# Two-layer hybrid mixer on one core: two-stream h slots, a new tile order in the first layer, earlier conversion of y

## The chip, the cores and the metric

The kernel runs on one core of a Trainium2 chip. The metric is the device time of one execution in microseconds (us). The profile is one execution taken apart by the hardware profiler: when each engine worked (TensorE = PE, VectorE = DVE, ScalarE = ACT, GpSimd = POOL, SyncE = SP) and which semaphore ended each wait.

## The reference

Two layers over two token streams of 256 tokens each, a context stream (s = 0) and a latent stream (s = 1), with model width 2048. Only the latent stream of the second layer is an output, so there the context needs keys and values alone.

```python
for l in range(DEPTH):                       # DEPTH = 2
    h  = layernorm(x)  * (1 + scale)   + shift        # latent, 256 x 2048
    hx = layernorm(ctx)* (1 + scale_x) + shift_x      # context
    qa, ka, va, za, qb, kb, vb, zb, qkv_c, zc, ab = split(h @ w_in)   # and the same of hx
    ya = attention(rope(rms(qa)), rope(rms(ka)), va; context keys first) * silu(za)   # 8 heads, 2 kv heads
    yb = neighbourhood_attention(qb, kb, vb, rpb) * silu(zb)                          # 4 heads
    yc = rms(bidirectional_gated_deltanet(conv(qkv_c), ab)) * silu(zc)                # 4 heads
    x  = layernorm(alpha * x + gate * (concat(ya, yb, yc) @ w_out))
    # context alike, but not in the last layer
```

## The kernel before

**Tiles.** `w_in` is cut in tiles of 128 columns, named by group and head: `("ck", 0)`, `("za", 3)`. A layer has 52 of them. The activations lie transposed, 16 pieces (`kt`) of 128 features by 512 tokens, context in columns 0 to 255 and latent in 256 to 511. To keep fp32 accuracy, each operand is two parts: a rounded high part and the rest. ACT (or DVE, by `high`) casts the high part, and DVE subtracts to get the low one (`wHL<-raw,wHL` in the rows). Each product is three matmuls: high by high, high by low, low by high. So a tile over both streams is 16 x 3 = 48 matmuls of 512 columns (`acc<-hH,wHL` and `acc<-hL,wHL`).

**Layers.** In the first layer (l = 0) all 52 tiles are of 512 columns. In the second, 32 tiles serve the latent stream alone (`LAT_ONLY`; 48 matmuls of 256 columns each) and 20 "shared" tiles (ck, cv, ka, va, kb, vb) serve both; there the two streams' h lie in different buffers of the ring `hp`, so `run_w` issues 96 matmuls of 256 columns for a shared tile. The tiles run in the order of `ORDER[l]`; behind each, a task (`evac`) takes it out of PSUM, and further tasks work on it: `attend` (scores, softmax, product with v, product with the gate's silu in `y`), and `delta` (the DeltaNet head: its triangular inverse in 31 dependent steps, a scan, the norm, and the product with silu(zc)).

**Output.** `convert` makes the high and low part (`yHL`) of each of the 16 finished heads y in the order `K_ORDER[l]`; 0 to 7 are A heads, 8 to 11 B, 12 to 15 the DeltaNet heads. `run_wo` then multiplies them with `w_out` in column blocks nb of 512: the `o<-wHL,yHL` matmuls, three for each head, block of 128 tokens and nb. The normalised result is h of the next layer.

**Order of work.** A program at build time, class `Order`, steps all tasks by a model of each engine's time and so writes out one fixed order of instructions for each engine. Each engine then works strictly in its order. `mod_dve` is filler on DVE: 512 products (`gvj<-gvl,xsb,modT` and `gvl<-…`) for the second layer's modulation, issued where the model finds DVE free. Weights come on the SP queue as `raw`; the bias tables `tbm` and the gate rows `gscr<-mrow` go through POOL's queue, `tbm` behind `gscr<-mrow`.

The end of the last weight tile in the main loop, before the change:

```python
if it[2] == ORDER[l][-1]:
    for k in range(4):
        hp.put(2)
    if it[3][1] == KT:
        if l == 0:
            layer_params(1)
        od.spawn(convert(l))
```

A tile runs as four groups of four kt (`it[3]` is the range of kt, `KT` is 16), so `convert` starts behind the last group. `md<-gvr,xs` is a modulation product that stands between the last tile and the first output matmul in both layers.

Of the kernel before, what the change touches and what calls it, by code (L numbers as in the profile page):

```python
# [7 lines left out]
F32 = mybir.dt.float32  # L8
# [8 lines left out]
KT = 16  # L17
# [47 lines left out]
def _b(*hs):  # L65
# [9 lines left out]
    [("ck", 0), ("cv", 0), ("cq", 0), ("ka", 0), ("ka", 1), ("zc", 0), ("va", 0), ("va", 1)] + _REST,  # L75
# [5 lines left out]
    [12, 0, 1, 2, 13, 3, 4, 5, 6, 14, 7, 8, 9, 15, 10, 11],  # L81
# [179 lines left out]

class Eng:
# [60 lines left out]
def hybrid_grid_flow(  # L323
# [15 lines left out]
    hp = Ring(od, big, "h", 32)  # L339
    yq = Ring(od, big, "yq", 18)  # L340
# [145 lines left out]
    def split_ahead(force=None):  # L486

        low_parts(force)
        while pos["split"] < len(queue):
            it = queue[pos["split"]]  # L490
            if it[0] in ("w", "wo"):
# [5 lines left out]
                if it[0] == "wo" and it[1] == DEPTH - 1 and it[3] == 3:  # L497
                    rings += [P_r, hp]
# [211 lines left out]
    for l in range(DEPTH):  # L710
        L[l] = dict(hs={}, xn={}, ln_ok=[Flag() for _ in range(4)], gates=Flag(), h_lat=Flag(), y={}, yp={}, yh={}, y_ok={})
# [12 lines left out]
    def h_run(l, streams, xn, ab_ps, wab):  # L724

        hs, mt = L[l]["hs"], modT[l]
# [7 lines left out]
        def turn():  # L734
# [11 lines left out]
            a = yield from hp.get("hH", dt=F32R)  # L746
            b = yield from hp.get("hL", dt=F32R)
            high(a, hf)
            V.tensor_tensor(b, hf, a.bitcast(F32), op=ALU.subtract)
            for i, kt in enumerate(kts):  # L750
                if both:
                    hs[kt] = [(slice(0, 512), a, b)]
                    hfs[kt] = hf
                else:
                    s, c = streams[0], slice(i * 256, i * 256 + 256)
                    hs.setdefault(kt, []).append((slice(s * 256, s * 256 + 256), a[:, c], b[:, c]))
                    hfs[kt] = hf[:, c]
# [313 lines left out]
    def attend(l, kind, h, q, rs, tbm=None):  # L1071
# [3 lines left out]
        while not (kk in P and vk in P and yk in P["y"]):  # L1075
            yield 1.0
        k, v, yt = P[kk], P[vk], P["y"][yk]
# [5 lines left out]
        left = [len(units)]  # L1083
        qs, ks, vs = (q, k, v) if two else ((q,), (k,), (v,))
        pairs = ((0, 0), (1, 0), (0, 1))[:3 if two else 1]

        def soft(tts, out):
# [6 lines left out]
            for i, t in enumerate(tts):  # L1094
                for n, (a, b) in enumerate(pairs):
                    T.matmul(sc[:, i * nk:(i + 1) * nk], qs[a][:, t * 128 - q0:t * 128 - q0 + 128], ks[b][:, 0:nk],
                             start=(n == 0), stop=(n == len(pairs) - 1))
            yield
# [27 lines left out]
        def one(tts):  # L1126
# [50 lines left out]
            yield  # L1177
            c = slice(tts[0] * 128 - y0, tts[0] * 128 - y0 + w)
# [3 lines left out]
            if not left[0]:  # L1182
                yq.put(2 if two and not l else 1)
                P["y_ok"][yk] = 1
# [36 lines left out]
    def delta(l, h):  # L1221
# [146 lines left out]
        for i in range(31):  # L1368
# [6 lines left out]
            yield 0  # L1375
            V.tensor_tensor(R[:, i + 1:32, 0:c_], R[:, i + 1:32, 0:c_], t, op=ALU.add)
            yield 0
# [158 lines left out]
        yield  # L1536
        pt = yield from tr.get("otr")
# [3 lines left out]
        while 12 + h not in P["y"]:  # L1541
            yield 1.0
        yt = P["y"][12 + h]
# [27 lines left out]
    def run_w(it):  # L1571
# [3 lines left out]
        if k0 == 0:  # L1575
# [7 lines left out]
            {c[0].start // 256 for c in P["hs"].get(k, ())} >= (set(streams) if l else {0})  # L1583
# [32 lines left out]
    def convert(l):  # L1616
        P = L[l]
        for n, k in enumerate(K_ORDER[l]):
# [38 lines left out]
    def run_wo(it):  # L1657
# [25 lines left out]
        def mults(s, i, yt, wh, wl, first, last_):  # L1683
            c = slice(i * 128, i * 128 + 128)
            ps = op["ps", nb, s][i]
            T.matmul(ps, yt[:, 0, c], wh, start=first, stop=False)
            T.matmul(ps, yt[:, 1, c], wh, start=False, stop=False)
            T.matmul(ps, yt[:, 0, c], wl, start=False, stop=last_)
# [14 lines left out]
        else:  # L1703
            w_free(it)
            if nb == 3:
                hp.put()
# [324 lines left out]
```

## Time and profile before

| | |
|---|---|
| time before, 3 runs | 1749.89, 1753.56 and 1754.09 us, median 1753.56 us |
| profiled execution: its own time | 1746.19 us |
| its span (first to last instruction) | 1744.4 us |
| mean granted TensorE clock | 0.99 of full |
| PE busy | 1664.7 us (95%) |
| DVE busy | 1307.4 us (75%) |
| ACT busy | 856.0 us (49%) |
| DMA | 296.43 MB, mean 170 GB/s |

The first layer's tiles run to about 846 us, its output matmuls to about 1053 us, the second layer's tiles to 1630 us, and its output matmuls to the end. "Busy" of matmuls is modelled and overlaps from one matmul to the next, so the price of one matmul is better read from the distance between starts in an unbroken run.

### The profile page before, as it was taken

To read this page: it belongs to the slowest core of one execution; us is meant where nothing else is said; L and a number is where in the kernel's file an instruction comes from. 1 tells how busy PE (TensorE), PEld (TensorE's weight loads), DVE (VectorE), ACT (ScalarE), POOL (GpSimd) and SP (SyncE) were. 2 spreads that over 40 slices of the span, in tenths; PEclk is the share of its full clock that TensorE was granted. 3 is DMA by queue.
4 is the path that set the end of the run, shared out by engine and by line. 5 is a ranking of instruction groups with operands and counts; after the bars stand their busy time and mean duration, and the time that the engine had idled before them with its cause. 6 is when DMAs were issued, how large, how long until landed. Compare 5 with 4: busy or idle time off the path is not lost. (4 is left out here: it accounts for less than half of the span.)

```text
span 1744.4 us, 32868 instructions
## 1 busy us (share of the span) xinstructions
PE 1664.7 (95%) x11487; PEld 1390.7 (80%) x11487; DVE 1307.4 (75%) x3948; ACT 856.0 (49%) x1932; POOL 42.7 (2%) x112
## 2 busy tenths in 40 slices
PE   4999999999999999999899898999999999999896
PEld 1667778787787878877688677898999899999785
DVE  5346787988798987868886788658788777685667
ACT  2225455364555443534444465545675655545443
POOL 0000100000000000000000000000000000000000
PEclk9999999999999999999999999999999999999998
DMA  9993544554455555454557767345454534353475
GB/s 322 347 348 100 158 144 120 164 166 146 125 157 161 162 153 171 135 178 127 165 182 231 254 222 217 98 128 146 130 163 139 149 98 141 114 159 119 145 233 182
DMA packets 213493, 296.43 MB, mean 170 GB/s; under 512 B 38384, under 2 KB 104656, under 8 KB 213328
## 3 DMA queue, kind: packets, MB, share of 16 engines
q1 hardware_dynamic: 211632, 291.07, 54.8%
q0 software_dynamic: 1696, 3.27, 0.6%
q8 instruction: 90, 1.47, 0.3%
q14 instruction: 75, 0.61, 0.1%
HBM read 287.88 MB, written 6.37 MB: 169 GB/s over the span
## 5 line engine op out<-in xcount | busy, mean ns | idle before, releaser
L307 PE MATMUL acc<-hH,wHL 128*128 128x256 f32 (+1 forms) x3968 | 1026.4, 338 | 8.8 <-DVE wHL L288 5.7
L307 PEld LDWEIGHTS acc<-hH,wHL 128*128 128x128 f32 x3968 | 683.1, 190 | 108.9 <-issue 26.4
L307 PE MATMUL acc<-hL,wHL 128*128 128x256 f32 (+1 forms) x1984 | 651.2, 328 | 0.2 <-DVE hL L288 0.2
L288 DVE TENSOR_TENSOR wHL<-raw,wHL 128x512 fp32r<-128x512 f32 (+1 forms) x610 | 403.0, 672 | 86.4 <-ACT wHL L288 71.9
L288 ACT ACTIVATE wHL<-raw 128x512 fp32r<-128x512 f32 (+1 forms) x524 | 311.1, 611 | 209.4 <-PE o L307 59.0
L307 PEld LDWEIGHTS acc<-hL,wHL 128*128 128x128 f32 x1984 | 378.3, 191 | 31.3 <-issue 3.4
L307 PE MATMUL o<-wHL,yHL 128*128 128x512 f32 x1152 | 275.1, 397 | 11.4 <-DVE yHL L288 4.8
L307 PEld LDWEIGHTS o<-wHL,yHL 128*128 128x128 f32 x1152 | 217.6, 191 | 62.9 <-DVE wHL L288 6.9
L288 DVE CUSTOM_DVE_ANT_0 gvl<-gvl,xsb,modT 128x256 f32<-128x256 f32 x224 | 109.5, 489 | 11.9 <-DMA xsb<-xsd 6.9
L288 DVE CUSTOM_DVE_ANT_0 gvj<-gvl,xsb,modT 128x256 f32<-128x256 f32 x224 | 107.3, 479 | 7.1 <-DMA xsb<-xsd 5.4
L307 PE MATMUL md<-gvr,xs 128*32 128x128 f32 (+1 forms) x1408 | 88.7, 350 | 24.7 <-DMA gvr<-in_w_mod_dram 24.0
L288 ACT ACTIVATE P<-P,zz 128x512 f32<-128x512 f32 (+1 forms) x61 | 39.4, 658 | 98.4 <-DVE zz L288 98.4
L307 PEld LDWEIGHTS md<-gvr,xs 128*32 128x32 f32 x1408 | 33.0, 113 | 64.5 <-DMA gvr<-in_w_mod_dram 27.8
L288 DVE TENSOR_TENSOR Xt<-X,R 128x60 f32<-128x60 f32 (+24 forms) x248 | 52.3, 211 | 9.4 <-ACT X L288 3.9
L288 DVE TENSOR_TENSOR R<-R,Xt 128x60 f32<-128x60 f32 (+24 forms) x248 | 52.8, 213 | 5.8
L307 PE MATMUL pv<-PT,v 128*128 128x128 f32 (+1 forms) x288 | 52.0, 296 | 0.0
L288 DVE SCALAR_TENSOR_TENSOR cv<-acc,cw,cv 128x510 f32<-128x510 f32 (+1 forms) x48 | 33.7, 703 | 22.3 <-ACT cv L288 21.3
L288 DVE TENSOR_REDUCE mx<-sc 128x1 f32<-128x512 f32 (+1 forms) x60 | 41.2, 687 | 6.3 <-PE sc L307 5.5
L307 PEld LDWEIGHTS pv<-PT,v 128*128 128x128 f32 x288 | 42.3, 191 | 3.5 <-ACT P L288 0.4
L288 DVE DVE_READ_ACCUMULATOR2_ANT modT<- 128x1 f32 x512 | 43.5, 85 | 0.0
L288 ACT ACTIVATE PT<-ptr 128x512 f32<-128x512 f32 (+1 forms) x54 | 32.1, 594 | 22.9 <-PE ptr L317 22.5
L288 ACT ACTIVATE P<-sc,nb,rqs 128x512 f32<-128x512 f32 (+1 forms) x48 | 33.6, 703 | 15.7 <-DVE nb L288 15.3
(294 smaller groups left out, 1783.6 us busy)
## 6 DMA issues: line engine op xcount, KB each, us to landing
raw<-in_w_in_dram SPq DMA_DIRECT2D x398, 256.0 KB
gvr<-in_w_mod_dram SPq DMA_DIRECT2D x256, 256.0 KB
raw<-in_w_out_dram SPq DMA_DIRECT2D x176, 256.0 KB
gvl<-in_w_modt_dram SPq DMA_DIRECT2D x256, 128.0 KB
raw<-in_w_in_dram SPq DMA_DIRECT2D x36, 128.0 KB
xp<-in_xin_dram SPq DMA_DIRECT2D x16, 256.0 KB
E<-growd SPq DMA_DIRECT2D x16, 256.0 KB
xres<-in_xin_dram SPq DMA_DIRECT2D x16, 256.0 KB
```

What stands on the lines that cost most here:

```text
L288: r = fn(*a, **k)
L307: r = self.real.matmul(out, lhsT, rhs, **k)
```

## The change

It does these things:

1. `ORDER[0]` is rewritten: B heads stand among the first layer's middle tiles, A heads 4 to 6 behind them, and the last tiles are qa7, za7, zc3, so two gates are last. `K_ORDER[0]` follows.
2. In layer 1 the h of both streams lies in one set of 32 slots `hv` (class `Slots`, each half of a slot booked by itself), context in columns 0 to 255 and latent in 256 to 511; a shared tile is then 48 matmuls of 512 columns. `convert` writes the parts of y into freed slots of the same set. A ring `Spare` over slots 16 to 31 takes the place of `hp` for the last output weights.
3. `h_run` writes high and low parts kt by kt: in layer 1 two pieces of 256 columns in place of one of 512.
4. `attend` no longer waits for its gate's y before the scores, only before the last product, and frees y's ring entry once the scores are issued.
5. In the inverse of `delta`, the product and the addition of a step are issued as a pair.
6. `delta` waits for its gate before it takes the PSUM tile of the transposes `otr`, and no longer behind them.
7. `convert` starts behind the first of the last tile's four groups.

```diff
 ORDER = (
-    [("ck", 0), ("cv", 0), ("cq", 0), ("ka", 0), ("ka", 1), ("zc", 0), ("va", 0), ("va", 1)] + _REST,
+    [("ck", 0), ("cv", 0), ("cq", 0), ("ka", 0), ("ka", 1), ("zc", 0), ("va", 0)]
+    + _a(0, 1, 2) + _c(1) + _a(3) + [("zc", 1)] + _b(0) + _c(2) + _b(1) + [("zc", 2)] + _b(2) + _c(3) + _b(3) + [("va", 1)] + _a(4, 5, 6)+ [("qa", 7), ("za", 7), ("zc", 3)],
     [("cq", 0), ("zc", 0), ("za", 0), ("zc", 1), ("za", 1), ("za", 2), ("ck", 0), ("cv", 0), ("ka", 0), ("va", 0)]
     + [("ka", 1), ("va", 1)]
     + [k for k in _REST if k not in [("zc", 1), ("za", 0), ("za", 1), ("za", 2)] + _KV1],
 )
 K_ORDER = (
-    [12, 0, 1, 2, 13, 3, 4, 5, 6, 14, 7, 8, 9, 15, 10, 11],
+    [12, 0, 1, 2, 13, 3, 8, 9, 14, 10, 11, 4, 5, 6, 15, 7],
     [12, 0, 1, 2, 13, 3, 4, 5, 6, 14, 7, 8, 9, 10, 11, 15],
...
+class Slots:
+
+
+    def __init__(self, order, n):
+        self.order, self.t = order, [None] * n
+        self.busy, self.times = set(), {}
+
+    def take(self, keys):
+        self.busy.update(keys)
+
+    def get(self, keys):
+        while True:
+            t = max(self.times.get(k, 0.0) for k in keys)
+            if any(k in self.busy for k in keys):
+                yield Want(self, keys)
+            elif t > self.order.t["PE"]:
+                yield ("at", t)
+            else:
+                return self.take(keys)
...
-            a = yield from hp.get("hH", dt=F32R)
-            b = yield from hp.get("hL", dt=F32R)
-            high(a, hf)
-            V.tensor_tensor(b, hf, a.bitcast(F32), op=ALU.subtract)
+            if both:
+                h2 = []
+                for nm in ("hH", "hL"):
+                    h2.append((yield from hp.get(nm, dt=F32R)))
+            else:
+                yield from hv.get([(2 * kt + j, streams[0]) for kt in kts for j in range(2)])
+            cols = slice(streams[0] * 256, streams[-1] * 256 + 256)
+            w = cols.stop - cols.start
             for i, kt in enumerate(kts):
-                if both:
-                    hs[kt] = [(slice(0, 512), a, b)]
-                    hfs[kt] = hf
-                else:
-                    s, c = streams[0], slice(i * 256, i * 256 + 256)
-                    hs.setdefault(kt, []).append((slice(s * 256, s * 256 + 256), a[:, c], b[:, c]))
-                    hfs[kt] = hf[:, c]
+                hfs[kt] = hf[:, i * w:i * w + w]
+                P["ht"][kt] = h2 if both else hv.t[2 * kt:2 * kt + 2]
+                high(P["ht"][kt][0][:, cols], hfs[kt])
+            for kt in kts:
+                a, b = P["ht"][kt]
+                V.tensor_tensor(b[:, cols], hfs[kt], a[:, cols].bitcast(F32), op=ALU.subtract)
+                hs[kt] = hs.get(kt, set()) | set(streams)
...
-        while not (kk in P and vk in P and yk in P["y"]):
+        while not (kk in P and vk in P):
             yield 1.0
-        k, v, yt = P[kk], P[vk], P["y"][yk]
+        k, v = P[kk], P[vk]
...
+            scored[0] -= len(tts)
+            if not scored[0]:
+                yq.put(2 if two and not l else 1)
...
+            while yk not in P["y"]:
+                yield 0.3
+            yt = P["y"][yk]
...
                 op=ALU.mult,
             )
-            yield 0
             V.tensor_tensor(R[:, i + 1:32, 0:c_], R[:, i + 1:32, 0:c_], t, op=ALU.add)
-            yield 0
+            if i % 1 == 0:
+                yield 0
...
+        while 12 + h not in P["y"]:
+            yield 0.5
+        yt = P["y"][12 + h]
         pt = yield from tr.get("otr")
         for n in range(n0, 4):
             T.transpose(pt[:, blk[n]], o2[:, blk[n]], ident)
         tmp.put()
-        while 12 + h not in P["y"]:
-            yield 1.0
-        yt = P["y"][12 + h]
...
-            parts = [c for c in P["hs"][kt] if l == 0 or c[0].start // 256 in streams]
-            for i, (c, a, b) in enumerate(parts):
-                T.matmul(ps[:, c], wh[:, w], a, start=(kt == 0 and i == 0), stop=False)
-                T.matmul(ps[:, c], wh[:, w], b, start=False, stop=False)
-                T.matmul(ps[:, c], wl[:, w], a, start=False,
-                         stop=(kt == KT - 1 and i == len(parts) - 1))
+            a, b = (t[:, lo:512] for t in P["ht"][kt])
+            T.matmul(ps[:, lo:512], wh[:, w], a, start=(kt == 0), stop=False)
+            T.matmul(ps[:, lo:512], wh[:, w], b, start=False, stop=False)
+            T.matmul(ps[:, lo:512], wl[:, w], a, start=False, stop=(kt == KT - 1))
...
-                t = yield from hp.get("yHL", dt=F32R, shape=[128, 2, 256])
                 c = slice(s * 256, s * 256 + 256) if l == 0 else slice(0, 256)
-                high(t[:, 0], y[:, c])
-                V.tensor_tensor(t[:, 1], y[:, c], t[:, 0].bitcast(F32), op=ALU.subtract)
+                if l == 0:
+                    if s:
+                        for j in range(2):
+                            hv.t[2 * n + j] = yield from hp.get("hv", dt=F32R)
+                    yield from hv.get([(2 * n + j, s) for j in range(2)])
+                    t = [hv.t[2 * n + j][:, c] for j in range(2)]
+                else:
+                    yield from hv.get(hv.whole(n))
+                    t = [hv.t[n][:, 0:256], hv.t[n][:, 256:512]]
+                high(t[0], y[:, c])
+                V.tensor_tensor(t[1], y[:, c], t[0].bitcast(F32), op=ALU.subtract)
...
-                for k in range(4):
-                    hp.put(2)
-                if it[3][1] == KT:
-                    if l == 0:
-                        layer_params(1)
+                if l == 0:
+                    hp.put(8)
+                else:
+                    hv.put([k for i in range(2 * it[3][0], 2 * it[3][1]) for k in hv.whole(i)])
+                    if it[3][1] == KT:
+                        spare.open(od.t["PE"])
+                if it[3][0] == 0:
                     od.spawn(convert(l))
+                if it[3][1] == KT and l == 0:
+                    layer_params(1)
```

**PE, a shared tile of the second layer.** `abtok` and `ab` are small products of the gates; `acc` is the tile. Before:

```order
L307 MATMUL acc<-hH,wHL 128x256 x2
L307 MATMUL acc<-hL,wHL 128x256
L307 MATMUL acc<-hH,wHL 128x256
L307 MATMUL abtok<-cst,abpart 128x16 x4
L307 MATMUL acc<-hH,wHL 128x256
L307 MATMUL acc<-hL,wHL 128x256
L307 MATMUL acc<-hH,wHL 128x256 x2
```

Now:

```order
L367 MATMUL acc<-hv,wHL 128x512 x18
L367 MATMUL ab<-hf,wab 32x256 x4
L367 MATMUL acc<-hv,wHL 128x512 x6
L367 MATMUL abtok<-cst,abpart 128x16 x4
L367 MATMUL acc<-hv,wHL 128x512 x24
```

In place of 96 matmuls of 256 columns a shared tile has 48 of 512; over the 20 shared tiles that is 1920 before and 960 now.

**PE, the end of the first layer's tiles.** `otr` are the transposes of the last DeltaNet head's output `o`, `ptr` and `pv` the transposes of an attention head's probabilities and their product with v, `sc` scores. Before:

```order
L307 MATMUL md<-gvr,xs 32x256 x4
L307 MATMUL sc<-kb,qb 128x512
L317 MATMUL otr<-cst,o_9450 128x128 x4
L307 MATMUL o<-wHL,yHL 128x512 x12
L307 MATMUL sc<-kb,qb 128x512
L307 MATMUL sc<-kb,qb 128x256 x2
L307 MATMUL o<-wHL,yHL 128x512 x9
L317 MATMUL ptr<-cst,P 128x128 x4
```

Now:

```order
L367 MATMUL md<-gvr,xs 32x256 x4
L377 MATMUL ptr<-cst,P 128x128 x4
L367 MATMUL pv<-PT,v 128x256 x2
L377 MATMUL otr<-cst,o_9458 128x128 x4
L367 MATMUL o<-wHL,hv 128x512 x645
L377 MATMUL htr<-cst,res 128x128 x8
```

The scores of the last B head are gone from here; the last piece of a head's attention (`ptr`, `pv`) stands between `md` and `otr`, and behind `otr` come output matmuls alone.

**ACT at the same place, now.** `se` are the three steps of the last gate's silu, `PT` the copy of `ptr` that `pv` reads, `o_9458` the operand of `otr`:

```order
L348 ACTIVATE hv<-y 128x256 x4
L348 ACTIVATE wHL<-raw 128x512
L348 ACTIVATE ory<-orv 128x4
L348 ACTIVATE ory<-ory 128x4
L348 ACTIVATE se<-acc 128x512
L348 ACTIVATE se<-se,cst 128x512
L348 ACTIVATE se<-se 128x512
L348 ACTIVATE PT<-ptr 128x512
L348 ACTIVATE o_9458<-O,c_osc 128x128 x4
```

The conversions `hv<-y` now come ahead of the last gate's silu, and the PT copy and the operand of `otr` behind it.

**PE, the end of the second layer's tiles.** `sc` are the last B head's scores. Before:

```order
L307 MATMUL md<-gvr,xs 32x256 x4
L307 MATMUL o<-wHL,yHL 128x512 x3
L307 MATMUL sc<-H,qb 128x512 x2
L307 MATMUL sc<-L,qb 128x512
L307 MATMUL sc<-H,qb 128x512 x2
L307 MATMUL sc<-L,qb 128x512
L307 MATMUL o<-wHL,yHL 128x512 x42
```

Now:

```order
L367 MATMUL md<-gvr,xs 32x256 x4
L367 MATMUL o<-wHL,hv 128x512 x21
L367 MATMUL sc<-H,qb 128x512 x2
L367 MATMUL sc<-L,qb 128x512
L367 MATMUL sc<-H,qb 128x512 x2
L367 MATMUL sc<-L,qb 128x512
L367 MATMUL scan<-vw,E 128x128 x2
L367 MATMUL o<-wHL,hv 128x512 x36
L377 MATMUL ptr<-cst,P 128x128 x4
```

Twenty-one output matmuls now stand ahead of the scores, where three stood.

**DVE at the same place, now.** `mrow` goes to POOL's queue, `tbm` comes from it; `wHL` rows are low parts of weights:

```order
L348 TENSOR_TENSOR hv<-y,hv 128x256 x3
L348 TENSOR_TENSOR wHL<-raw,wHL 128x512
L348 SCALAR_TENSOR_TENSOR rr<-scan,g_neg_eg_12468,vn 128x128 x2
L348 TENSOR_TENSOR wHL<-raw,wHL 128x512
L348 SCALAR_TENSOR_TENSOR cv_16822<-scan,g_eg_12469,cv_16822 128x128 x2
L348 TENSOR_TENSOR mrow<-md,gb 128x256
L348 SCALAR_TENSOR_TENSOR qb<-acc,qb 128x256
L348 TENSOR_TENSOR tbm<-tbm,cst 128x384
L348 TENSOR_TENSOR wHL<-raw,wHL 128x512 x3
L348 TENSOR_TENSOR hv<-y,hv 128x256
```

The low parts of the first three converted heads stand ahead of `tbm`; before, the first of them stood directly behind it. The fourth stands behind `tbm` and three low parts of weights.

## Rows read from the trace of the kernel before

**Rows 1.** Windows by stage: busy us and instructions of each engine, PEclk, DMA share.

```profile
660.00:800.00 140.00, 139.99 (x799) 112.68 (x797) 108.70 (x403) 61.57 (x147) 4.18 (x8) 1.00 0.54 160
...
846.00:858.00 12.00, 6.14 (x24) 3.58 (x23) 9.74 (x39) 2.82 (x9) 1.72 (x3) 0.72 0.49 146
...
1120.00:1360.00 240.00, 235.89 (x2041) 223.41 (x2043) 182.82 (x536) 140.12 (x336) 6.95 (x20) 1.00 0.47 136
...
1630.00:1644.00 14.00, 9.02 (x37) 6.75 (x30) 8.63 (x21) 4.68 (x12) 1.72 (x3) 0.76 0.35 115
```

**Rows 2.** Chain that ended last: start us, us, engine, operation, line, count; unbroken runs.

```profile
1432.12 6.83 PE acc L307 x57
...
1539.16 11.52 PE acc L307 x96
...
1659.18 26.69 PE o L307 x117
```

**Rows 3.** Timeline of PE, first and last row of an unbroken run (512 columns).

```profile
207.21 0.61 PE L307 MATMUL acc<-hH,wHL 128*128 128x512 f32 x2
...
216.05 0.61 PE L307 MATMUL acc<-hH,wHL 128*128 128x512 f32 x2
```

**Rows 4.** Timeline of PE, first layer's end: start, us, instruction, [idle before, releaser].

```profile
753.85 0.62 PE L307 MATMUL acc<-hH,wHL 128*128 128x512 f32 x2
...
846.70 0.64 PE L307 MATMUL md<-gvr,xs 128*32 128x256 f32 x8
849.27 1.13 PE L307 MATMUL sc<-kb,qb 128*128 128x512 f32 x2 [1.93 <-ACT qb L288]
854.33 1.36 PE L317 MATMUL otr<-cst,o 128*128 128x128 f32 x4 [3.93 <-ACT o L288]
855.34 4.29 PE L307 MATMUL o<-wHL,yHL 128*128 128x512 f32 x12
859.47 1.88 PE L307 MATMUL sc<-kb,qb 128*128 128x512 f32 x6
```

**Rows 5.** Timeline of ACT at the same place.

```profile
843.07 1.94 ACT L288 ACTIVATE yHL<-y 128x256 fp32r<-128x256 f32 x6
...
848.62 0.60 ACT L288 ACTIVATE qb<-acc 128x512 f32<-128x512 f32 x1 [1.76 <-DVE yHL L288]
853.87 1.28 ACT L288 ACTIVATE o<-O,c_osc 128x128 f32<-128x128 f32 x4 [4.66 <-DVE c_osc L288]
```

**Rows 6.** Timeline of DVE at the same place.

```profile
847.78 2.09 DVE L288 TENSOR_TENSOR yHL<-y,yHL 128x256 fp32r<-128x256 f32 x6
```

**Rows 7.** Timeline of PE, second layer's end.

```profile
1629.76 0.64 PE L307 MATMUL md<-gvr,xs 128*32 128x256 f32 x8
1630.61 0.50 PE L307 MATMUL o<-wHL,yHL 128*128 128x512 f32 x1 [0.21 <-ACT yHL L288]
1635.88 1.22 PE L307 MATMUL o<-wHL,yHL 128*128 128x512 f32 x2 [4.77 <-DVE yHL L288]
...
1639.45 9.88 PE L307 MATMUL o<-wHL,yHL 128*128 128x512 f32 x42
```

**Rows 8.** Timeline of DVE at the same place.

```profile
1634.93 0.56 DVE L288 TENSOR_TENSOR tbm<-tbm,cst 128x384 f32<-128x384 f32 x1 [3.68 <-DMA tbm<-in_tb_dram]
```

**Rows 9.** Groups by line and shape: count, busy us, mean ns, idle before and releasers.

```profile
L288 DVE TENSOR_TENSOR wHL<-raw,wHL 128x512 fp32r<-128x512 f32 x574 | 388.7, 688 | 74.7 <-ACT wHL L288 64.3 <-PE o L307 2.7
...
L288 DVE CUSTOM_DVE_ANT_0 gvl<-gvl,xsb,modT 128x256 f32<-128x256 f32 x224 | 109.5, 489 | 11.9 <-DMA xsb<-xsd 6.9
...
L288 DVE TENSOR_REDUCE mx<-sc 128x1 f32<-128x512 f32 x48 | 33.0, 688 | 5.5 <-PE sc L307 4.8
...
L288 ACT ACTIVATE se<-se,cst 128x512 f32<-128x512 f32 x36 | 26.1, 724 | 1.2
L288 ACT ACTIVATE se<-se 128x512 f32<-128x512 f32 x36 | 22.8, 632 | 1.1
...
...
L288 ACT ACTIVATE PT<-ptr 128x512 f32<-128x512 f32 x36 | 21.4, 594 | 14.4 <-PE ptr L317 14.1
```

More of the change, by code (lines that the diff above doesn't have):

```diff
@@ L259, in get, with __init__, free, put @@
             yield self
+class Want(Flag):
+    def __init__(self, slots, keys):
+        self.slots, self.keys = slots, keys
+    @property
+    def free(self):
+        return not any(k in self.slots.busy for k in self.keys)
+class Slots:
[13 more added lines that the diff above has]
+                return self.take(keys)
+    def put(self, keys, t=None):
+        o = self.order
+        if t is None:
+            t = max(o.last.values()) if o.last else 0.0
+        for k in keys:
+            self.busy.remove(k)
+            self.times[k] = t
+    def whole(self, i):
+        return [(i, 0), (i, 1)]
+class Spare(Ring):
+    def __init__(self, order, slots, ids):
+        self.order, self.slots, self.ids, self.n, self.at = order, slots, list(ids), len(ids), 0
+        self.tag, self.times = "spare", []
+    def open(self, t):
+        self.times = [t] * self.n
+    def take(self, name, dt=F32, shape=None):
+        self.times.remove(min(self.times))
+        self.at += 1
+        return self.slots.t[self.ids[(self.at - 1) % self.n]]
 class Eng:
@@ L339, in hybrid_grid_flow @@
     hp = Ring(od, big, "h", 32)
+    hv = Slots(od, 32)
+    spare = Spare(od, hv, range(16, 32))
     yq = Ring(od, big, "yq", 18)
@@ L497, in split_ahead @@
                 if it[0] == "wo" and it[1] == DEPTH - 1 and it[3] == 3:
-                    rings += [P_r, hp]
+                    rings += [P_r, spare]
                 ts = sorted((t, i) for i, r in enumerate(rings) for t in r.times)[:2]
@@ L710, in hybrid_grid_flow @@
     for l in range(DEPTH):
-        L[l] = dict(hs={}, xn={}, ln_ok=[Flag() for _ in range(4)], gates=Flag(), h_lat=Flag(), y={}, yp={}, yh={}, y_ok={})
+        L[l] = dict(hs={}, xn={}, ln_ok=[Flag() for _ in range(4)], gates=Flag(), h_lat=Flag(), y={}, yp={}, yh={}, y_ok={}, ht={})
     wabs = {}
@@ L724, in h_run @@
     def h_run(l, streams, xn, ab_ps, wab):
-        hs, mt = L[l]["hs"], modT[l]
+        P, hs, mt = L[l], L[l]["hs"], modT[l]
         tts = [2 * s + i for s in streams for i in range(2)]
@@ L1083, in attend @@
         left = [len(units)]
+        scored = [sum(len(u) for u in units)]
         qs, ks, vs = (q, k, v) if two else ((q,), (k,), (v,))
@@ L1182, in one @@
             if not left[0]:
-                yq.put(2 if two and not l else 1)
                 P["y_ok"][yk] = 1
@@ L1582, in run_w @@
         od.until(lambda: all(
-            {c[0].start // 256 for c in P["hs"].get(k, ())} >= (set(streams) if l else {0})
+            P["hs"].get(k, set()) >= set(streams)
             for k in range(k0, k1)))
@@ L1685, in mults @@
             ps = op["ps", nb, s][i]
-            T.matmul(ps, yt[:, 0, c], wh, start=first, stop=False)
-            T.matmul(ps, yt[:, 1, c], wh, start=False, stop=False)
-            T.matmul(ps, yt[:, 0, c], wl, start=False, stop=last_)
+            T.matmul(ps, yt[0][:, c], wh, start=first, stop=False)
+            T.matmul(ps, yt[1][:, c], wh, start=False, stop=False)
+            T.matmul(ps, yt[0][:, c], wl, start=False, stop=last_)
         def out_of(s, tiles):
@@ L1704, in run_wo @@
             w_free(it)
-            if nb == 3:
-                hp.put()
+            if nb == 3 and l == 0:
+                hv.put([(2 * ki + j, ss[0]) for j in range(2)])
         advance()
```

## The prediction

> **What bounds the kernel now.** I read the windows by stage first, to see which engine a saved microsecond must be saved on. From 660 to 800 us PE works 139.99 of 140 us, and in the second layer's tiles 235.89 of 240, while DVE works 108.70 and 182.82 [rows 1]. So TensorE's rows set the time, and an edit pays in two ways only: fewer or cheaper matmuls, or a stretch in which PE stands idle. Of those stretches the windows show two that the diff touches, at the end of each layer's tiles: PE is busy 6.14 us of 12 at 846, and 9.02 of 14 at 1630, with the granted clock down to 0.72 and 0.76 [rows 1]. Then I read PE's timeline there, for what ended each wait. At the first layer's end PE waits 1.93 us for `qb` and 3.93 us for `o`, 5.86 us together [rows 4]; at the second's 0.21 and 4.77 us for parts of y, 4.98 together [rows 7]. The chain of waits gave the pace of unbroken runs [rows 2].
>
> **1. Shared tiles in 512 columns.** 57 matmuls of 256 columns took 6.83 us, 119.8 ns each; 96 took 11.52, 120.0 ns [rows 2]. Thirty-nine of 512 columns (13 periods of three) lie between 207.21 and 216.05, which is 226.7 ns each [rows 3]; 117 of the output took 26.69 us, 228.1 ns [rows 2]. Two of 256 cost 239.6, one of 512 226.7 to 228.1: 11.5 to 12.9 ns saved per pair. The change has 960 pairs (the first two order excerpts), so 11.0 to 12.4 us; I take **-12**. The lower bound is nothing, if another engine sets the pace of those tiles: DVE works 182.82 of 240 us there [rows 1], so it has no such claim on average.
>
> The Trainium skill (TensorE: Matmul & The Clock Gate, "Back-to-back issue gap") gives an isolated gap of N/2.4 + 2.5 ns at the full clock. By it a pair would save 2.5 ns, 2.4 us over 960. The rows disagree: they hold 13 ns per matmul beyond the columns' own time, since 256 columns more cost 226.7 - 119.8 = 106.9 ns [rows 2, 3].
>
> **2. The end of the first layer's tiles.** Before, ACT spends 1.94 us on six casts of y [rows 5] and DVE 2.09 us on their low parts [rows 6], between the last tile and the evacuation of `qb`; the norm of the DeltaNet head then reaches `otr` only at 854.33 [rows 4]. The change starts the conversion three groups (36 matmuls, 36 x 0.2267 = 8.2 us) earlier, and puts the last B head's attention far ahead. What takes the wait's place is in ACT's excerpt: the copy `PT` stands behind the three silu steps of the last gate, and `otr` waits for `o` behind that copy. The tile ends with the silu's input, `md` covers 0.6 us, and two steps of 0.724 and 0.632 and a first that I put at 0.6, like the copy, come to 1.95 us, the copy 0.594 [rows 9]; 2.55 in all; less the cover of `md` and, at most, 0.3 of `ptr`, 1.6 to 1.9 us, and some 0.5 for `o` behind it: 2.2 us in place of 5.86, so -3.7. Behind the old wait the clock was low: 12 output matmuls from 855.34 to 859.47 took 344 ns each against 226.7 [rows 4], 1.4 us, and `otr` some 0.5; a wait of 2.2 us should not bring that back, so -1.9 (bounds 0 and -1.9).
>
> Against it stands the load of the last six tiles. By the order, DVE has there 180 instructions before and 259 now; priced with each kind's mean, 71 us and 96 us. Most of the difference is 14 more modulation products (0.489 + 0.085 us each, 8 us), 9 more maxima (0.688, 6 us) and 7 more low parts of weights (0.688, 5 us) [rows 9]. PE gets about 100 small attention matmuls more there, by my estimate 10 us (0.1 each, the lower end of what a matmul of 256 columns or fewer takes [rows 2]) on top of the 92.6 us that these tiles took, from the second matmul of the row at 753.85 to `md` at 846.70 [rows 4]. So DVE has 96 us of work beside 103 of PE: it fits, but tightly, and the work comes in bursts. I charge **+2** (bounds 0 and +8). In turn the middle of the layer has less DVE work; at 660 to 800 PE is never idle [rows 1], so I take nothing (bounds -4 and +4). Sum of this part: **-3.6**, with -10 and +8 as its ends.
>
> **3. The end of the second layer's tiles.** PE waits there for a low part of y that stands behind `tbm` on DVE, and `tbm` ends its wait for a DMA at 1634.93 [rows 8], 4.53 us behind `md`'s end (1629.76 + 0.64) [rows 7]. That DMA is behind `mrow` on POOL's queue and `mrow` behind `md`; the change leaves this alone. What it changes is the cover: three low parts now stand ahead of `tbm`, so 18 output matmuls and one more can run, 19 x 0.228 = 4.3 us. The fourth low part stands behind `tbm` (0.56) and three low parts of weights (some 0.6 each), at about 4.5 + 0.6 + 1.8 + 0.4 = 7.3 us behind `md`. That leaves 7.3 - 4.3, between 2.8 and 3.0 us idle, in place of 4.98: -2.2. Before, two output matmuls and six scores from 1635.88 to 1639.45 took 446 ns each [rows 7], 1.75 us over the full pace; I take half back, -1.0 (bounds 0 and -1.9). New is a wait near the end of nb 0: `pv` of the last head stands behind 84 output matmuls, so head 11's product and parts may come late: +1.0 (0 to +2). Sum **-2.2** (-4 to +2).
>
> **4. The rest.** In layer 1 the low part of h costs DVE two subtracts of 256 columns in place of one of 512 (like a low part of weights, 0.688 us [rows 9]; six of 256 took 2.09, 0.35 each [rows 6]), so almost nothing; it is at the start of the layer, where h is waited for: +0.5 (0 to +1). The pairs of the inverse put two dependent DVE instructions next to each other more often; at an estimated 0.1 us more per step for the 62 steps or so whose neighbours change, up to 6 us over eight heads, spread under PE's tiles with DVE at three quarters [rows 1]: 0, and those 6 us if DVE were full there. Earlier scores and the earlier release of y's ring entry move no price of their own: 0. SP's loads are as many as before, and at PE's writes to `hv` the order adds no wait.
>
> **Sum.** -12 - 3.6 - 2.2 + 0.5 = -17.3 us. The profiled execution took 1746.19 us (span 1744.4 and 1.8 around it), so its like would take 1729; but the runs' median, 1753.56, lies 7.4 above it, and I set the forecast against that: **1736 us**. A difference under 0.3%, 5.3 us, can't be told from no change, so faster is below 1748.3 and slower above 1758.8.
>
> **Rivals.**
> *DVE sets the pace of the first layer's last six tiles.* For it: 96 us against 103 is the tightest load that I found, and the filler products are issued by a model that doesn't see small waits. Against it: DVE was at 108.70 of 140 with PE at 139.99 [rows 1], and PE did not wait. It would take 8 us of the gain: about 1744. Chance 0.20.
> *All of it comes, and more.* The lighter middle gives its 4 us, the rebuilt waits are covered, the clock stays up: -12.4 - 10 - 4 and some 2 of small waits, -28: about 1725. For it speaks that each wait named is one on an engine's order; against it that ACT's order shows the new wait in print. Chance 0.17.
> *A pair saves only 2.4 us in all.* Then -2.4 - 3.6 - 2.2 + 0.5 = -7.7: about 1746. Mechanism: the start of a second matmul would lie under the first one's columns, so halving the count saves no issue time. The rows at two sizes speak against it. The rule of the Trainium skill cited above is this case. Chance 0.05.
> *The 512-column tiles are quicker on PE but evacuation does not keep up.* In the second layer tiles of both streams end 12 us sooner in all, and ACT and DVE, which empty them and split weights, hold PE by as much; the layer ends gain no more than the last six tiles lose. About 1753. DVE's 182.82 of 240 us speaks against it. Chance 0.08.
> *Slower: a backlog on DVE at the first layer's end.* Low parts of weights stand in one order with products, maxima and conversions; if 25 us of moved-in work makes each of the last 24 groups' low parts late, PE waits at each group. It decides when these waits pass 17.3 + 5.3 = 22.6 us, about 1 us for each of the 24 groups: above 1759, say 1762. Against it: PE has 103 us of its own there, so some 30 us of DVE's 96 would have to fall where PE can't cover it. Chance 0.07.
>
> **How the numbers follow.** The forecast has 0.43, its own range 1730 to 1742. Faster: 0.43, 0.17 of the first rival, 0.17, 0.03 of the third: 0.80. Same: what is left of these two and the fourth, 0.13. Slower: 0.07. The range 1720 to 1749 leaves out the last two rivals and a tail of the second, not quite 0.2.
>
> **What would show it.** Right: in the changed profile shared tiles run at about 227 ns a matmul, no `acc` of 256 columns is left but for latent tiles, the second layer's tiles take some 12 us less; between `md` and the output matmuls of the first layer PE idles about 2 us, released by ACT, with the clock near 1; at the second layer's end the idle row shows about 3 us after 19 output matmuls. Wrong: idle of PE released by DVE's `wHL` before the first layer's last tiles (first and last rivals), or by ACT or DVE inside the second layer's shared tiles (the fourth), or a pace there that is near 237 ns (the third).

## The result, and the profile after

The changed kernel takes 1732.39 us (median of 4 runs, 1731.44 to 1734.63) against 1752.27 us before: ratio 0.9889, 95% interval 0.9874 to 0.9903, some 20 us faster. Timed a second time, beside the last experiments, it was 1731.83 us, ratio 0.9876 (0.9853 to 0.9898). The forecast was 1736 us, range 1720 to 1749.

The profiled execution took 1732.42 us, 13.8 less than that of before; the rest of the 20 us is that before's profiled execution was among its quickest (below). This is the head of the page of the changed kernel.

```profile
span 1730.6 us, 30951 instructions
...
PE 1657.6 (96%) x10527; PEld 1338.1 (77%) x10527; DVE 1321.0 (76%) x3973; ACT 852.9 (49%) x1939; POOL 43.0 (2%) x112
```

The windows of the changed kernel that answer to [rows 1]:

```profile
660.00:800.00 140.00, 139.99 (x836) 111.93 (x835) 119.06 (x449) 70.67 (x172) 3.58 (x7) 1.00 0.50 148
848.40:860.00 11.60, 9.91 (x50) 7.20 (x50) 11.32 (x42) 7.84 (x19) 1.16 (x2) 1.00 0.54 170
1120.00:1360.00 240.00, 234.32 (x1626) 202.61 (x1626) 185.72 (x536) 138.56 (x332) 6.58 (x19) 0.99 0.49 143
1616.00:1630.00 14.00, 10.30 (x46) 8.29 (x47) 9.02 (x23) 6.18 (x18) 1.57 (x3) 1.00 0.40 128
1634.00:1644.00 10.00, 9.54 (x51) 7.63 (x49) 7.05 (x19) 5.30 (x14) 0.00 (x0) 1.00 0.72 212
1644.00:1654.00 10.00, 9.28 (x33) 7.35 (x34) 6.41 (x12) 4.91 (x9) 0.00 (x0) 0.83 0.64 197
```

DVE has 119.06 us of work from 660 to 800 where it had 108.70, and PE is busy in every microsecond as before. At the first layer's end PE stands for 1.7 us of 11.6, with the clock at full. At the second layer's end the clock is full as well; it falls to 0.83, a mean of the full level (2.4 GHz) and the half one (1.2 GHz), from 1644 on, 20 us behind the long wait.

PE's timeline at the first layer's end, which answers to [rows 4]:

```profile
848.40 0.64 PE L367 MATMUL md<-gvr,xs 128*32 128x256 f32 x8
848.97 0.66 PE L377 MATMUL ptr<-cst,P 128*128 128x128 f32 x4
851.06 1.13 PE L367 MATMUL pv<-PT,v 128*128 128x256 f32 x4 [1.43 <-ACT PT L348]
852.45 1.21 PE L377 MATMUL otr<-cst,o 128*128 128x128 f32 x4 [0.26 <-ACT o L348]
853.42 8.91 PE L367 MATMUL o<-wHL,hv 128*128 128x512 f32 x38
```

And ACT's there ([rows 5]):

```profile
848.51 0.60 ACT L348 ACTIVATE se<-acc 128x512 f32<-128x512 f32 x1 [0.61 <-PE acc L367]
849.14 0.72 ACT L348 ACTIVATE se<-se,cst 128x512 f32<-128x512 f32 x1
849.89 0.63 ACT L348 ACTIVATE se<-se 128x512 f32<-128x512 f32 x1
850.43 0.58 ACT L348 ACTIVATE PT<-ptr 128x512 f32<-128x512 f32 x1
```

The new wait is where ACT's order put it: `pv` waits 1.43 us for the copy that stands behind three silu steps. The two waits sum to 1.69 us in place of 5.86.

PE's timeline at the second layer's end ([rows 7]), and then DVE's ([rows 8]):

```profile
1614.41 0.64 PE L367 MATMUL md<-gvr,xs 128*32 128x256 f32 x8
1614.98 4.89 PE L367 MATMUL o<-wHL,hv 128*128 128x512 f32 x19
1623.57 0.73 PE L367 MATMUL o<-wHL,hv 128*128 128x512 f32 x2 [3.69 <-DVE hv L348]
...
1643.48 0.28 PE L367 MATMUL pv<-PTL,v 128*128 128x256 f32 x1
1644.72 5.51 PE L367 MATMUL o<-wHL,hv 128*128 128x512 f32 x15 [0.96 <-ACT hv L348]
```

```profile
1620.81 0.56 DVE L348 TENSOR_TENSOR tbm<-tbm,cst 128x384 f32<-128x384 f32 x1 [4.92 <-DMA tbm<-in_tb_dram]
1621.29 1.89 DVE L348 TENSOR_TENSOR wHL<-raw,wHL 128x512 fp32r<-128x512 f32 x3
1623.09 0.42 DVE L348 TENSOR_TENSOR hv<-y,hv 128x256 fp32r<-128x256 f32 x1
```

Nineteen output matmuls run, then PE waits 3.69 us for the fourth head's low part, which stands on DVE behind `tbm` and three low parts of weights.

### The profile page after: what moved, and what is told of

Its sections match the earlier page's. It is cut to its first block, busy times and chain, and to the rows that moved or that the text cites. A ratio compares the mean times of both kernels' runs of the same rounds, so it can differ in the third digit from the quotient of the medians.

```text
span 1730.6 us, 30951 instructions
## 1 busy us (share of the span) xinstructions
PE 1657.6 (96%) x10527; PEld 1338.1 (77%) x10527; DVE 1321.0 (76%) x3973; ACT 852.9 (49%) x1939; POOL 43.0 (2%) x112
## 5 line engine op out<-in xcount | busy, mean ns | idle before, releaser
L367 PE MATMUL acc<-hH,wHL 128*128 128x512 f32 x1664 | 573.9, 407 | 0.7 <-ACT hH L348 0.5
L348 DVE TENSOR_TENSOR wHL<-raw,wHL 128x512 fp32r<-128x512 f32 (+1 forms) x600 | 396.3, 671 | 84.9 <-ACT wHL L348 67.0
L367 PE MATMUL acc<-hv,wHL 128*128 128x256 f32 (+1 forms) x2496 | 448.1, 332 | 10.3 <-DVE wHL L348 7.2
L367 PEld LDWEIGHTS acc<-hv,wHL 128*128 128x128 f32 x2496 | 369.4, 192 | 63.2 <-DVE wHL L348 9.3
L348 ACT ACTIVATE wHL<-raw 128x512 fp32r<-128x512 f32 (+1 forms) x511 | 302.7, 610 | 222.2 <-PE o L367 64.2
L367 PEld LDWEIGHTS acc<-hH,wHL 128*128 128x128 f32 x1664 | 312.5, 188 | 85.0 <-issue 18.2
L367 PE MATMUL acc<-hL,wHL 128*128 128x512 f32 x832 | 324.9, 390 | 0.2 <-DVE hL L348 0.2
L367 PE MATMUL o<-wHL,hv 128*128 128x512 f32 x1092 | 259.1, 396 | 9.5 <-DVE hv L348 3.7
L367 PEld LDWEIGHTS o<-wHL,hv 128*128 128x128 f32 x1092 | 206.4, 191 | 58.2 <-DVE hv L348 4.4
L367 PEld LDWEIGHTS acc<-hL,wHL 128*128 128x128 f32 x832 | 156.8, 189 | 30.6 <-issue 3.6
```

Source lines behind the costliest of these rows:

```text
L348: r = fn(*a, **k)
L367: r = self.real.matmul(out, lhsT, rhs, **k)
```

## The experiments

All stages of all profiles are cut at the same rows of PE's timeline: the start of `md` at the first layer's end, of the second layer's first `acc`, of `md` at the second layer's end, and the span's end. Before, these lie at 846.70, 1052.98, 1629.76 and 1744.4 us; in the changed kernel at 848.40, 1043.17, 1614.41 and 1730.6. The differences, in us, with one profile for each row:

| kernel | first layer's tiles | its output | second layer's tiles | its output | median us | ratio to before, 95% interval |
|---|---|---|---|---|---|---|
| before | 846.7 | 206.3 | 576.8 | 114.6 | 1752.27 | |
| before_again | 845.2 | 205.8 | 582.3 | 114.9 | 1749.86 (one run) | |
| slots_only | 849.6 | 207.1 | 568.9 | 114.8 | 1742.22 | 0.9945 (0.9929 to 0.9961) |
| slots_early | 846.6 | 207.8 | 570.3 | 114.4 | 1741.84 | 0.9930 (0.9909 to 0.9952) |
| old_order | 844.6 | 203.1 | 571.1 | 115.7 | 1736.87 | 0.9912 (0.9897 to 0.9928) |
| late_convert | 848.6 | 200.1 | 571.6 | 115.6 | 1738.87 | 0.9929 (0.9912 to 0.9945) |
| old_attend | 844.1 | 207.3 | 572.3 | 115.4 | 1739.60 | 0.9934 (0.9916 to 0.9951) |
| no_pair | 849.1 | 200.1 | 569.7 | 114.1 | 1732.08 | 0.9889 (0.9870 to 0.9907) |
| split256 | 848.9 | 194.9 | 579.0 | 114.7 | 1738.69 | 0.9925 (0.9912 to 0.9938) |
| split_first | 876.5 | 193.8 | 571.5 | 116.3 | 1761.60 | 1.0040 (1.0023 to 1.0057) |
| changed | 848.4 | 194.8 | 571.2 | 116.2 | 1732.39 | 0.9889 (0.9874 to 0.9903) |
| after_again | 846.8 | 196.1 | 571.7 | 115.6 | 1731.83 | 0.9876 (0.9853 to 0.9898) |
| tbm_before | 848.8 | 210.4 | 582.0 | 110.1 | 1750.88 | 0.9989 (0.9972 to 1.0005) |
| tbm_early | 847.9 | 191.9 | 570.8 | 108.3 | 1721.24 | 0.9827 (0.9809 to 0.9846) |

The experiments were timed in three groups, in which the kernel before had medians of 1750.76, 1751.48 and 1753.70 us. A difference of medians across groups can be off by as much, and the intervals of the ratios are 2 to 4 us to either side; so differences of 2 or 3 us between rows are not told apart from none.

**split256: the columns undone.**

```diff
-            T.matmul(ps[:, lo:512], wh[:, w], a, start=(kt == 0), stop=False)
...
+            cs = [slice(0, 512)] if l == 0 else [slice(x, x + 256) for x in range(lo, 512, 256)]
+            for i, c in enumerate(cs):
+                a, b = (t[:, c] for t in P["ht"][kt])
+                T.matmul(ps[:, c], wh[:, w], a, start=(kt == 0 and i == 0), stop=False)
...
```

> The changed kernel with one thing undone: a shared tile of the second layer is again 96 matmuls of 256 columns, from the same slots. Theory (a pair of 256 columns costs 12.9 ns more than one of 512, and PE sets the time of these tiles): 11 to 12.4 us slower than the changed kernel's 1732.4, so 1743 to 1745. Rival (only what the two profiled executions differ by between the second layer's first tile and its last, 577.0 against 571.5 us, comes from the columns): 5 to 6 us slower, 1738.

It was 1738.69 us, 6.3 over the changed kernel, and 7.8 us longer in the second layer's tiles (579.0 against 571.2). This is nearer the rival's number. A tile's same piece, with the same pauses, in the timelines of split256 and then of the changed kernel:

```profile
1125.75 6.71 PE L367 MATMUL acc<-hv,wHL 128*128 128x256 f32 x54
1132.39 0.64 PE L367 MATMUL md<-gvr,xs 128*32 128x256 f32 x8
```

```profile
1124.64 6.41 PE L367 MATMUL acc<-hv,wHL 128*128 128x512 f32 x27
1130.97 0.64 PE L367 MATMUL md<-gvr,xs 128*32 128x256 f32 x8
```

From start to `md` 6.64 us for 54 matmuls and 6.33 for 27: 11.5 ns per pair. So the price of a pair was right, and 960 of them are 11 us; 7.8 arrive. The pace of one matmul is as forecast too: the changed kernel's chain of work has 27 of them in 6.14 us, 227.4 ns each:

```profile
1540.64 6.14 PE acc L367 x27
```

Part of the rest shows as waits: all waits of PE in this stage sum to 16.4 us in split256 and 18.9 in the changed kernel. Their largest rows, in that order (us in total, times, longest):

```profile
PE acc L367 <- DVE wHL L348: 5.6, 3, 4.7
```

```profile
PE acc L367 <- DVE wHL L348: 7.2, 8, 4.8
```

Eight waits for low parts of weights stand where three stood: 1.6 of the 2.5 us by which the waits are longer; the rest is waits of 0.6 us or less on other tiles, less one of 1.1 us that is gone. The 2.5 us are most of the 3.2 missing; what the last 0.7 is stays open, all the more as the clock differs by 1.8 us between the two profiles (under before_again below).

**split_first: the same edit where nothing else moves much.**

```diff
+            cs = [slice(x, x + 256) for x in range(lo, 512, 256)] if l == 0 else [slice(lo, 512)]
```

> The changed kernel with the first layer's tiles as matmuls of 256 columns too, 4992 in place of 2496; the second layer's shared tiles stay at 512. It has 2.6 times the pairs of the change's edit and TensorE is busy all through. Theory (a pair costs 12.9 ns as in unbroken runs): 32 us slower than the changed kernel, 1764. Rival (what all rows of the shared tiles showed, 241.0 against 231.7 us and 239.3 against 231.3, 8 to 9.6 ns a pair, because short pauses in the order make up part of it): 20 to 24 us, 1753 to 1756. If the pairs cost only what the whole time moved with split columns, 6.3 us for 960: 16 us, 1749.

29.8 us over after_again, timed beside it, for 2496 pairs: 11.9 ns a pair, near the theory's end. By the first layer's tiles it is 28.1 or 29.7 us, by which profile of the changed kernel one takes. In these tiles, where PE hardly waits (6.2 us from 120 to 870), the price of a pair arrives nearly in full.

**slots_only: the slots and the columns on the kernel before.** Edits 2 and 3 stay; edits 1 and 4 to 7 are undone, as in the experiments below.

> The kernel before with the slots and the 512-column shared tiles alone: old order of the first layer, conversion behind the last tile, old waits in the attention and in the DeltaNet head, no pairs. Theory: 11 to 12.4 us faster than before, ratio 0.993 to 0.994. Rival: 5 to 6 us, ratio 0.9966.

Ratio 0.9945, 8.5 us in medians, between theory and rival, with 568.9 us in the second layer's tiles against 576.8 and 582.3. That is 7.9 or 13.4 us less, by which profile of before one takes; the clock's spread between those two is told below. The interval holds the theory's ratios and leaves out the rival's 0.9966. So on the kernel before all 11 us may arrive; the loss is shown beside the other edits only, by split256.

**old_order: the first layer's order of before.**

```diff
-    [("ck", 0), ("cv", 0), ("cq", 0), ("ka", 0), ("ka", 1), ("zc", 0), ("va", 0)]
...
+    [("ck", 0), ("cv", 0), ("cq", 0), ("ka", 0), ("ka", 1), ("zc", 0), ("va", 0), ("va", 1)] + _REST,
```

> The changed kernel with the first layer's tile order and head order of before; early conversion stays. Theory (the new order and the early conversion together took 4 to 5 us of idle time and clock from the first layer's end, and the early conversion alone can't, because the last B head's scores and products stand there again): 3 to 6 us slower than the changed kernel. Rival (the order only moves DVE work about, and early conversion gave the gain): within 1.5 us of it.

It is 4.5 us slower than the changed kernel in medians, as the theory said (the two intervals overlap a little), but not by its mechanism. At the layer's end this kernel hardly waits:

```profile
844.62 0.64 PE L366 MATMUL md<-gvr,xs 128*32 128x256 f32 x8
845.66 1.20 PE L376 MATMUL otr<-cst,o 128*128 128x128 f32 x4 [0.41 <-ACT o L347]
...
857.33 3.02 PE L366 MATMUL o<-wHL,hv 128*128 128x512 f32 x12 [0.28 <-DVE hv L347]
861.61 4.60 PE L366 MATMUL o<-wHL,hv 128*128 128x512 f32 x19 [1.25 <-DVE hv L347]
```

Waits for late heads follow inside the output stage instead (3.0 us in all), and that stage, which still holds the last B head's scores, is 8.3 us longer (203.1 against 194.8) where its tiles are 3.8 shorter.

**late_convert: the conversion behind the last tile.**

```diff
-                if it[3][0] == 0:
-                    od.spawn(convert(l))
-                if it[3][1] == KT and l == 0:
-                    layer_params(1)
+                if it[3][1] == KT:
+                    if l == 0:
+                        layer_params(1)
+                    od.spawn(convert(l))
```

> The changed kernel with the conversion of y behind the last tile, as before. Theory: at the second layer's end three low parts fall behind the bias table's wait again, which costs 2.7 us there (16 of the 19 covering matmuls gone would be 3.6 us), and at the first layer's end six casts and low parts stand between the tile and the first output matmul, 1 to 3 us: 4 to 6 us slower than the changed kernel. Rival (other engines' work covers it): under 1.5 us slower.

6.5 us slower, a little over the theory, but all of it in the first layer: the output stage is 5.3 us longer, the second layer's end no longer at all (115.6 against 116.2). `otr` again waits 3.35 us for `o`, which on ACT stands behind five conversions, as the row of ACT shows below PE's:

```profile
848.59 0.64 PE L367 MATMUL md<-gvr,xs 128*32 128x256 f32 x8
852.58 1.35 PE L377 MATMUL otr<-cst,o 128*128 128x128 f32 x4 [3.35 <-ACT o L348]
...
856.28 10.05 PE L367 MATMUL o<-wHL,hv 128*128 128x512 f32 x36 [1.06 <-DVE y L348]
```

```profile
850.62 1.62 ACT L348 ACTIVATE hv<-y 128x256 fp32r<-128x256 f32 x5
```

**old_attend: the old waits of the attention and of the DeltaNet head.**

```diff
-        while not (kk in P and vk in P):
+        while not (kk in P and vk in P and yk in P["y"]):
...
         for n in range(n0, 4):
             T.transpose(pt[:, blk[n]], o2[:, blk[n]], ident)
         tmp.put()
+        while 12 + h not in P["y"]:
+            yield 1.0
```

> The changed kernel with the old waits: the scores of a head wait for its gate, y's ring entry is freed at the head's end, and the DeltaNet head takes its transposes' PSUM tile before it waits for its gate. Theory (with the gates last the last A head's scores now can't start before its gate's tile, so softmax and products of head 7 fall behind the first layer's last tile): 3 to 6 us slower than the changed kernel, as idle time between the last tile and the output matmuls. Rival (the waits have no price): within 1.5 us.

7.2 us slower, over the theory's range; edits 4 and 6 are undone together here, so their shares are not known. With the gates last, the last A head's scores start late, and its `ptr`, which waits for the softmax, stands ahead of `otr` and of the output matmuls:

```profile
844.06 0.64 PE L367 MATMUL md<-gvr,xs 128*32 128x256 f32 x8
851.57 1.11 PE L377 MATMUL ptr<-cst,P 128*128 128x128 f32 x4 [6.87 <-ACT P L348]
```

**no_pair: the inverse steps apart.** A `yield 0` stands again between the product and the addition.

> The changed kernel with the product and the addition of an inverse step issued apart again. Theory (the pairs are spread under TensorE's work): within 1.5 us of the changed kernel's 1732.4. Rival (the pairs are the 2.2 to 2.3 us by which the second layer's tiles are longer in the changed kernel than in the kernel with the slots alone, 571.5 against 569.2 us, and with split columns against the kernel before, 579.3 against 577.0): 2 us faster than the changed kernel, with 569 us there.

1732.08 us, the same. But the stages differ both ways: with the steps apart the first layer is 6.1 us longer (849.1 + 200.1 against 848.4 + 194.8; `otr` waits 4.70 us for `o`), the second layer's tiles 1.5 shorter and its output 2.1. So in these profiles the pairs finish the last DeltaNet head sooner and cost 3.6 us later; neither theory had said that. The profiled execution of no_pair was the slowest of its five, 2.6 us over the median, which is about what the two sides differ by.

**slots_early: early conversion alone on the slots.** Edits 1 and 4 to 6 are undone, edit 7 stays.

> The kernel with slots alone (1742.2) and the early conversion of y added; old order of the first layer, old waits, no pairs. Theory (early conversion frees the first layer's end by itself, as the 0.41 us of idle there with the old order showed): 4 to 6 us faster than with slots alone, 1736 to 1738. Rival (it needs the attention's new waits too): under 2 us.

1741.84 against 1742.22 us in medians, nothing. The two were timed in different groups, though; by their ratios, 0.9930 and 0.9945, it is 2.6 us, with intervals that overlap. So the rival is the likelier, but 4 us are not excluded. In the profile the early conversion lets the last B head's `ptr` move ahead of `otr` in PE's order, and that waits for the softmax:

```profile
846.55 0.64 PE L366 MATMUL md<-gvr,xs 128*32 128x256 f32 x8
847.37 1.12 PE L366 MATMUL sc<-kb,qb 128*128 128x512 f32 x2 [0.18 <-ACT qb L347]
854.82 1.12 PE L376 MATMUL ptr<-cst,P 128*128 128x128 f32 x4 [6.32 <-ACT P L347]
```

With the slots alone `otr` came first, behind a shorter wait:

```profile
857.18 1.35 PE L376 MATMUL otr<-cst,o 128*128 128x128 f32 x4 [3.90 <-ACT o L347]
```

**tbm_early: the bias table loaded a tile sooner, at the changed kernel.** `ev_v` of a B head issues the load, `ev_qb` only adds the mask.

```diff
+        if key[0] == "vb":
+            tbm = lay.tile([128, 384], F32, tag="tbm", name="tbm")
+            G.dma_start(tbm, tb[l, :, key[1]])
+            L[l]["tbm", key[1]] = tbm
...
-        G.dma_start(tbm, tb[l, :, h])
```

> The changed kernel with the bias table of a B head loaded when its v is done, a tile earlier, so that its load no longer stands behind the gate rows on POOL's queue at the second layer's end. Theory (the 3.69 us idle row there is ended by the low part behind that table): the row falls to under 1 us, 3 to 5 us faster than the changed kernel, 1728 to 1729. Rival (low parts of weights and the scores' chain take the wait's place): under 1.5 us faster.

1721.24 us, 11.1 less than the changed kernel, more than theory or rival said. The end stage fell from 116.2 to 108.3 us; PE's timeline there:

```profile
1610.63 0.64 PE L367 MATMUL md<-gvr,xs 128*32 128x256 f32 x8
...
1614.35 4.50 PE L367 MATMUL o<-wHL,hv 128*128 128x512 f32 x19
1619.32 0.74 PE L367 MATMUL o<-wHL,hv 128*128 128x512 f32 x2 [0.47 <-DVE hv L348]
```

POOL's timeline of the changed kernel, then of this one, shows the load behind the gate rows and 47 us ahead of them:

```profile
1615.86 1.16 POOL L348 DMA_DIRECT2D gscr<-mrow  x2 [90.28 <-DVE mrow L348]
1617.01 0.57 POOL L348 DMA_DIRECT2D tbm<-in_tb_dram  x1
```

```profile
1565.25 0.54 POOL L348 DMA_DIRECT2D tbm<-in_tb_dram  x1 [47.49 <-DVE sc L348]
1612.08 1.16 POOL L348 DMA_DIRECT2D gscr<-mrow  x2 [46.29 <-DVE mrow L348]
```

The wait of 3.69 us is 0.47, and the clock stays at full from 1612 to 1695 us. So the load behind the gate rows on POOL's queue held the second layer's end. Of the 7.9 us there, 3.2 are this idle and 1.6 the clock: the 204 output matmuls that took 48.69 us take 47.13. The rest was not taken apart. The other 3 us are in the first layer's output stage, where this kernel's order has no `ptr` and `pv` in front of `otr`; that these make them was not tested.

**tbm_before: the same at the kernel before.**

> The kernel before with the earlier load of the bias table alone. Theory (the table's load behind the gate rows made the 5 us of idle at the second layer's end, and the half clock behind it another 1.9): 5 to 8 us faster than before, ratio 0.9955 to 0.997. Rival (there the low parts of y are late in any case, since their conversion begins behind the tile): under 3 us, ratio above 0.998.

Ratio 0.9989 (0.9972 to 1.0005). The end stage is 4.5 us shorter (110.1 against 114.6) and its wait of 4.77 us is 0.99, so the theory's place is right; but the first layer with its output is 6 to 8 us longer (1059.2 against 1053.0 and 1051.0). There the last B head's `ptr` stands ahead of `otr`, and PE waits 5.58 us for its softmax, as in slots_early:

```profile
858.64 1.11 PE L317 MATMUL ptr<-cst,P 128*128 128x128 f32 x4 [5.58 <-ACT P L288]
...
1643.53 0.73 PE L307 MATMUL o<-wHL,yHL 128*128 128x512 f32 x2 [0.99 <-DVE yHL L288]
```

**before_again and after_again: second profiles.**

> The kernel before once more, for a second profile: the first one took 1746.19 us where the timed runs of it have a median of 1752. Theory: the 4 to 6 us lie in TensorE's clock and in waits of a us or so all over, not in one stage. Rival: in one of the two layer ends that the change touches, so that the change's gain there was read too small.

> The changed kernel once more, timed in the same rounds as these three and with a second profile. All theories: 1731 to 1735. By its stages it tells how far one profile of the same program lies from another: under 2.5 us a stage.

Both profiles of the changed kernel agree within 1.7 us a stage. Those of before differ in one, the second layer's tiles, 576.8 and 582.3 us; neither theory named it. It is the clock, not idle time. PE's waits in this stage sum to 17.4 and 17.0 us. In 58 equal windows of the stage, each one's length times what its granted clock lacks of full sums to 3.4 us in the first profile and 11.9 in the second. (The same sum is 8.4 us in slots_only, 8.5 in split256, 6.7 and 8.5 in the two profiles of the changed kernel, so stages of single profiles compare to within a few us.) The windows behind the wait for `HL`, in the first profile and then in the second:

```profile
1213.00:1223.00 10.00, 8.51 (x66) 8.30 (x67) 8.48 (x33) 4.93 (x12) 0.73 (x5) 1.00 0.20 57
```

```profile
1213.00:1223.00 10.00, 8.88 (x48) 8.41 (x49) 8.52 (x33) 5.29 (x13) 0.73 (x5) 0.66 0.10 29
```

The wait is 2.7 us in both; 66 matmuls fit in the 10 us behind it in the one, 48 in the other.

## Why the prediction was right, and which terms were not

The forecast of -17.3 us is near the measured -20, but three of its four terms were mis-sized, and their errors cancel. The mechanisms of the first two terms came, that of the third only in part, and that the sum is within 3 us is partly luck.

**Shared tiles, -12.** The price per pair was right (11.5 ns in the aligned piece, 11.9 in split_first). What went wrong is that all of it would reach the end, because "DVE works 182.82 of 240 us" on average. In the finished kernel 6.3 us of time do, 7.8 by the stage (split256); PE's waits there give 2.5 us back, and 1.6 of these are eight waits for low parts of weights in place of three. An average of 76% on DVE does not say that each low part is early enough for tiles that are 0.6 us shorter. On the slots alone (slots_only) no such loss is shown.

**First layer's end, -3.6.** The first layer, tiles and output together, ended 8 to 10 us sooner (1052.98 and 1050.99 before, 1043.17 and 1042.97 after). Idle went as forecast (1.69 us, forecast 2.2) and the clock stayed full. The +2 for DVE's load did not come. From 738 us to the layer's end, about the last six tiles, DVE works 91.78 of 110.40 us, a load near the forecast's 96 of 103; but from 660 us to the layer's end the view of PE's waits has no row, though the profile before had two waits there, of 1.42 and 1.57 us:

```profile
816.59 0.71 PE L307 MATMUL scan<-rr,W 128*128 128x128 f32 x4 [1.42 <-DVE rr L288]
...
834.48 1.16 PE L307 MATMUL scan<-S,cv 128*128 128x128 f32 x8 [1.57 <-DVE O L288]
```

I had left these out of the sum as not touched; with the moved attention work they are gone. I take that, and the last head's scores and products gone from the output stage, as the reason why the tiles are only 1.7 us longer with that work in them and the output 11.5 us shorter; it was not tested by itself. The edits behind it depend on each other: undone one at a time, the order lengthens the first layer by 4.5 us, the early conversion by 5.5, the pairs by 6.1 and the new waits by 8.2, together far more than the 8 to 10 gained. In time the early conversion is worth 6.5 us here and the new waits 7.2, while on the slots alone the early conversion gave 0.4 to 2.6 us, not told apart from nothing. I had priced the earlier scores at nothing; beside the new order that was wrong.

**Second layer's end, -2.2.** The stage became 0.7 to 1.6 us longer, not shorter. The cover of 19 matmuls and the 0.96 us wait for head 11 came as forecast. But the load of `tbm` ended 5.8 us behind `md`, not 4.5, so 3.69 us of idle remained. POOL issued it 1.96 us behind `md`'s end in both kernels. From there to DVE's use of it passed 2.6 us in both profiles of before and 3.8 and 4.0 in those of the changed kernel; why stays open. And the half clock came all the same, later (0.83 from 1644 to 1654 us) or right behind the wait (0.91 from 1616 to 1634 in the second profile); and four `scan` and two `otr` moved into this stage. late_convert shows that the conversion bought nothing here, and tbm_early that the table's load was what held this stage.

**The rest, +0.5.** By the profiles the pairs cost 1.5 to 2 us in each later stage and gave 6.1 us in the first layer; in medians they are worth nothing, so zero was right as a sum and wrong as a reason.

Of the rivals, DVE as the bound of the first layer's last tiles did not come, nor the backlog, nor the gain of 28 us; the one with 2.4 us for all pairs is excluded by split_first. Of the fourth, engines that hold PE in the second layer's tiles, some came: the 2.5 us of longer waits.

## What to carry to other kernels

Price a matmul edit from aligned pieces of both traces, but expect that part of it may be lost (here 11 us became 6 to 8) where another engine feeds the same matmuls just in time. When an idle stretch sits behind a load, look at what stands ahead of that load on its queue before moving the work that waits: the earlier load gave 7.9 us at the second layer's end, where the earlier conversion of y gave nothing. Edits that reorder one boundary should be tested in the order they will live in, because the early conversion gave 6.5 us beside the new order and waits and nothing that could be measured without them.

## What was not expected of the hardware

The same program, with the same 2.7 us wait, had the full clock behind it in one profile and 0.66 of it in another; it is part of the 5.5 us by which the two profiles' stages differ. In the changed kernel a wait of 3.69 us was followed by a full clock for 20 us, and a shorter one of 0.96 us then by 0.83 of it over 10 us; in its second profile 0.91 from 1616 to 1634 stood at the longer wait. So what a wait costs in clock is read as a spread over profiles, not from one.
